# Pair products: background steps bound behind sums and results, low parts written in place

## The chip, the cores and the metric

The kernel runs on one core of a Trainium2 chip. The metric is the device time of one execution in microseconds (us). Three executions of the kernel before took 1269.88 to 1273.23 us, with a median of 1271.97 us.

## The reference

One layer of an encoder trunk, for 1024 tokens of width 1024, all in float32. Cut to what matters:

```python
h    = rmsnorm(x) * g_pre_mix
proj = h @ w_in                       # 512 columns each: u_pool, q, k, v
# pooling: 4 groups of 128 columns, trailing windows of 2, 4, 8, 16 tokens
pooled = window_mean(u_pool) - u_pool            # per group
y_pool = (pooled @ w_pool_mix[g]) * pool_scale   # per group, then @ w_br_pool
# stick-breaking attention, 8 heads of 64, q scaled by 1/8
o_sb  = stick_breaking_attention(q, k, v)        # then @ w_br_sb
gates = sigmoid(h @ w_gate + b_gate)             # 2048 columns
m     = (gates[:, :1024] * y_pool + gates[:, 1024:] * y_sb) @ w_out
x     = x + rmsnorm(m) * g_post_mix
h2    = rmsnorm(x) * g_pre_mlp
out   = x + rmsnorm(relu(h2 @ w_up)**2 @ w_down) * g_post_mlp
```

## The kernel before, in words

Each float32 operand is split into a high and a low part in a rounded float32 format, and a product is the sum of three matmuls: high by high, low by high, high by low (lines 110 to 112). The phases follow one another: the norm and the first projections (u_pool and v), then the **pair stage** in `phase_project`, which the change touches, then attention, the output products and the MLP.

**Pair products.** The pair stage computes the gates and q and k. The list `PAIRS` has twelve pairs of weight blocks in this order: gates 0 to 4, q0, k0, q1, k1, gates 5 to 7. By a scheme of Winograd's kind a pair takes seven products (b11, b21, t2, t3, t1, t4, b22) rather than eight, each of twelve matmuls into one PSUM bank of 128x512, so 84 products. The operands on the activation side (h_hi, ht_hi and their like in the profile) are ready; those on the weight side are prepared pair by pair.

**Sums and results.** `begin` copies b11 to the tile u on ScalarE (line 683) and adds b21 to get c11 (line 684). The other sums, on VectorE (lines 695 to 705), make u, v and c22 from the products, always in float32 tiles of 128x512; u has two buffers and c11, v and c22 one each. Four of these tiles are results of a pair. `result` (from line 534) takes them on: a gate's result is put through the sigmoid in place on ScalarE and stored from ScalarE's DMA queue to gscr. A result of q or k is scaled and rounded to its high part on ScalarE (line 542), its low part is made on VectorE (line 543), both in a staging tile with room for the two (`staged`: the tags m0 and m1 in turn), and GpSimd's DMA queue stores them to qscr.

**Banks.** `newbank` deals the PSUM banks out in a cycle over three tags with 2, 2 and 3 buffers, so that a bank comes round after six or nine products. In the profile these banks are named sw.

**Weights.** `sw_weights` (from line 505) is a generator, advanced by one step after each product of the pair in front. It loads two raw tiles of 512 KB from SyncE's queue (wraw, with two buffers, and wrawx, with one), and splits them: the high part is a cast on ScalarE (line 1193), the low part a subtraction on VectorE (line 1194). Three sums of raw blocks (lines 519, 521 to 523) come between. The parts of a1 and sa are named whi and wlo in the profile, those of a22 a0hi and a0lo or a1hi and a1lo, those of sb s0hi, s0lo, s1hi, s1lo, by odd and even pair.

**Background steps.** `later` (from line 551) is a second generator, for work that is not of the pairs. One step of it is traced after each product, and one more after every sixth product among the first 36. It begins with four pooling groups. For a group it loads u on ScalarE's queue (line 560), builds the window sums by doubling (lines 581 and 582, tiles named win), makes the mean less u (lines 586 to 590), splits that (ph on ScalarE, line 594, and pq on VectorE, line 595), multiplies it by the group's mixing matrix into the bank dm and one more bank of the cycle, scales both into win and u (line 602 on ScalarE, line 603 on VectorE) and stores these to yscr from GpSimd's queue (line 610). All its big tiles share four buffers of 512 KB, tags m0 to m3. Then come eight value steps: each loads a tile of values and its neighbour shifted by one token (vpair), subtracts them (line 622), splits the difference (line 625 on ScalarE, line 626 on VectorE) and stores it to sscr (line 627). The value steps work in the tags m2 and m3 (m0 and m1 for two of them), so that m0 and m1 are free for the staging tiles of q and k.

**What sets the order.** Work is traced in the order of the program, and a scheduler then puts each engine's instructions in an order by its own simulated timeline. On the chip each engine, and each DMA queue, executes in that order; what stands behind a waiting instruction waits too. `tc.issue_after(ins)` (with a helper named `behind`) ties what is traced under it: on the engine of `ins` it stands behind `ins` in the order. In the kernel before, the pair stage ties nothing of the background and of the weights in this way. After the last pair the first head's tiles are loaded into the same four buffers, and attention begins.

## Time and profile before

| | value |
|---|---|
| median of 3 executions | 1271.97 us (1269.88 to 1273.23) |
| the profiled execution's own time | 1273.34 us |
| its span in the profile | 1271.3 us |
| TensorE (PE) busy | 1241.4 us, 98% |
| VectorE (DVE) busy | 967.8 us, 76% |
| ScalarE (ACT) busy | 631.0 us, 50% |
| GpSimd (POOL) busy | 179.7 us, 14% |
| chain that ended last | PE 69%, DVE 13%, DMA 10%, issue 5%, ACT 3% |

The profile is one execution, taken by the hardware profiler. A row of its groups gives the line and engine, the operation with the tiles it writes and reads, its count, the time it was busy, the mean of one, and the idle time ahead of it with what ended most of that. In a table by stretch the columns after the stretch are its length, then the busy time of PE, PE's weight loads, DVE, ACT and POOL, each with its number of instructions in brackets; then the clock granted to PE as a share of the full one, the mean busy share of the sixteen DMA engines, and GB/s. In a row of a timeline the start and the duration stand first, and in square brackets the time that the instruction's engine waited and for what. Rows of waits give the waiting operation, what it waited for, and total, count and longest. Rows of DMA issues give the queue, the count, the size of one, and the median time from issue to landing.

### The profile page before, as it was taken

Reading aid. Unit: us, or ns where it says so; the run is one execution under the profiler, and the core shown is the slowest. Engines: PE = TensorE matmul, PEld = TensorE weight load, DVE = VectorE, ACT = ScalarE, POOL = GpSimd, SP = SyncE. Lnnn points to the kernel's source line nnn. Section 1 sums busy time; section 2 is a strip of 40 time slices with the busy share of each in tenths; the row PEclk is TensorE's granted clock in tenths of the full one; section 3 lists DMA queues with packets and bytes.
Section 4 is the critical chain, followed back from the end, with each engine's and each line's share of the span. In section 5 each row is a group of like instructions: output and inputs, shape, how many; then the busy total and the mean of one; then the engine's idle time right before and its main releaser. Section 6 shows DMA issues by size and latency. Waiting matters only on the chain.

```text
span 1271.3 us, 16191 instructions
## 1 busy us (share of the span) xinstructions
PE 1241.4 (98%) x5707; PEld 1020.3 (80%) x5707; DVE 967.8 (76%) x1311; ACT 631.0 (50%) x1010; POOL 179.7 (14%) x319
## 2 busy tenths in 40 slices
PE   9999999998999999999999999999999999999998
PEld 6887778877877888787778878888888888888887
DVE  8849687766578898877797879887865565776975
ACT  8147334333456666674556546455454443344452
POOL 1212112342101111101100002222121110001000
PEclk9999999999999999999999999999999999999999
DMA  6586878977899674457648677676559996556552
GB/s 218 172 226 165 249 189 252 314 240 247 294 359 345 203 213 118 117 129 219 215 135 263 198 248 257 226 241 221 180 182 335 306 300 229 197 198 248 191 198 67
DMA packets 110305, 283.00 MB, mean 223 GB/s; under 512 B 12464, under 2 KB 17584, under 8 KB 109072
## 3 DMA queue, kind: packets, MB, share of 16 engines
q1 hardware_dynamic: 65696, 165.28, 37.9%
q0 software_dynamic: 30992, 91.13, 25.1%
q10 hardware_dynamic: 13536, 25.57, 6.2%
q8 instruction: 45, 0.74, 0.2%
q14 instruction: 36, 0.29, 0.1%
HBM read 208.52 MB, written 94.37 MB: 238 GB/s over the span
## 4 chain that ended last, share of the span: by engine, by line
PE 69%; DVE 13%; DMA 10%; issue 5%; ACT 3%; POOL 0%; ACTq 0%; SPq 0%; DVEq 0%; POOLq 0%
PE d L110 15%; PE d L111 15%; PE d L112 15%; PE sw L110 3%; PE sw L111 3%; PE sw L112 3%; PE o L838 2%; DVE T L801 2%; PE dbr L111 2%; PE dbr L112 2%; PE dbr L108 2%; DVE wlo L78 1%; DMA yscr<-win 1%; DMA wraw<-w 1%; PE at L814 1%
## 5 line engine op out<-in xcount | busy, mean ns | idle before, releaser
L111 PE MATMUL d<-blo,whi 128*128 128x512 f32 (+1 forms) x456 | 172.3, 378 | 0.0
L112 PE MATMUL d<-bhi,wlo 128*128 128x512 f32 (+1 forms) x456 | 171.9, 378 | 0.0
L110 PE MATMUL d<-bhi,whi 128*128 128x512 f32 (+1 forms) x456 | 168.7, 378 | 0.0
L112 PEld LDWEIGHTS d<-bhi,wlo 128*128 128x128 f32 x456 | 85.8, 188 | 16.1
L111 PEld LDWEIGHTS d<-blo,whi 128*128 128x128 f32 x456 | 85.7, 188 | 15.8
L110 PEld LDWEIGHTS d<-bhi,whi 128*128 128x128 f32 x456 | 85.5, 188 | 16.0
L801 DVE TENSOR_TENSOR_SCAN T<-T,past 128x512 f32<-128x512 f32 (+3 forms) x64 | 84.8, 1345 | 8.7 <-ACT T L799 8.4
L111 PE MATMUL d<-b_lo,whi 128*128 128x512 f32 x196 | 76.2, 390 | 1.2 <-DVE b_lo L1085 1.2
L110 PE MATMUL d<-b_hi,whi 128*128 128x512 f32 x196 | 75.7, 390 | 0.1
L112 PE MATMUL d<-b_hi,wlo 128*128 128x512 f32 x196 | 74.2, 389 | 0.0
L78 DVE TENSOR_TENSOR wlo<-wraw,whi 128x1024 fp32r<-128x1024 f32 x45 | 54.9, 1220 | 15.2 <-ACT whi L76 13.5
L76 ACT CAST whi<-wraw 128x1024 fp32r<-128x1024 f32 x45 | 47.5, 1056 | 37.9 <-DMA wraw<-w 19.0
L1382 DVE TENSOR_TENSOR wlo<-slots_hi,whi 128x1024 fp32r<-128x1024 f32 x29 | 35.5, 1223 | 37.3 <-ACT whi L1380 37.3
L1380 ACT CAST whi<-slots_hi 128x1024 fp32r<-128x1024 f32 x29 | 30.5, 1051 | 67.2 <-PE d L111 61.0
L799 ACT ACTIVATE T<-z 128x256 f32<-128x256 f32 (+2 forms) x96 | 44.8, 492 | 38.1 <-PE z L797 34.9
L1380 ACT CAST whi<-slots_lo 128x1024 fp32r<-128x1024 f32 x27 | 28.4, 1054 | 60.6 <-PE d L111 50.3
L110 PE MATMUL sw<-h_hi,whi 128*128 128x512 f32 x144 | 56.5, 392 | 1.9 <-DVE c L684 1.3
L111 PE MATMUL sw<-h_lo,whi 128*128 128x512 f32 x144 | 56.1, 389 | 0.0
L112 PE MATMUL sw<-h_hi,wlo 128*128 128x512 f32 x144 | 55.5, 390 | 0.1
L824 ACT CAST ahi<-at 128x512 fp32r<-128x512 f32 (+1 forms) x96 | 44.1, 484 | 22.8 <-PE at L814 19.8
L825 DVE TENSOR_TENSOR alo<-at,ahi 128x512 fp32r<-128x512 f32 (+1 forms) x96 | 50.0, 542 | 6.7 <-ACT ahi L824 6.6
L1193 ACT CAST whi<-wraw 128x1024 fp32r<-128x1024 f32 (+1 forms) x29 | 26.7, 928 | 54.7 <-PE d L111 24.2
(447 smaller groups left out, 3451.6 us busy)
## 6 DMA issues: line engine op xcount, KB each, us to landing
wraw<-w SPq DMA_DIRECT2D x57, 512.0 KB, 5.0
ext_b<-ascr SPq DMA_DIRECT2D x40, 512.0 KB, 7.0
wscr<-w POOLq DMA_DIRECT2D x32, 512.0 KB, 9.6
slots_hi<-w SPq DMA_DIRECT2D x10, 1024.0 KB, 8.0
slots_lo<-w SPq DMA_DIRECT2D x10, 1024.0 KB, 8.6
qq<-qscr SPq DMA_DIRECT2D x32, 256.0 KB, 5.1
pscr<-p SPq DMA_DIRECT2D x32, 256.0 KB, 3.9
u<-pscr ACTq DMA_DIRECT2D x32, 256.0 KB, 4.3
```

What stands on the lines that cost most here:

```text
L76: nc.scalar.copy(hi, raw)
L78: self.lows.append(nc.vector.tensor_sub(lo, raw, hi.bitcast(F32)).ins)
L110: nc.tensor.matmul(ps, wh, rh, start=first and i == 0, stop=False)
L111: nc.tensor.matmul(ps, wh, rl, start=False, stop=False)
L112: self.last_mm = nc.tensor.matmul(ps, wl, rh, start=False, stop=last and i == n - 1).ins
L799: self.after = nc.scalar.activation(f, z[:, :n], AF.Sigmoid, scale=-1.0)
L801: nc.vector.tensor_tensor_scan(f[:, ::-1], f[:, ::-1], past[:, ::-1], 1.0, ALU.mult, ALU.max)
L824: self.att_hi = nc.scalar.copy(hi[:, c:], at[:, c:]).ins
L825: self.att_lo = nc.vector.tensor_sub(lo[:, c:], at[:, c:], hi[:, c:].bitcast(F32)).ins
L1193: self.last_hi = nc.scalar.copy(hi, src).ins
L1380: last_split[0] = nc.scalar.copy(hi, src).ins
L1382: last_split[1] = nc.vector.tensor_sub(lo, src, hi.bitcast(F32)).ins
```

## The change

It has three parts, all in the pair stage.

First, the background steps are **bound**: each is now traced under `behind`, once for the last main instruction on ScalarE (the copy of b11 or the last result) and once for the last main sum on VectorE. On these two engines a step's instructions stand behind the copies, results and sums of the products in front. The weights' step comes after it and stays unbound, as it was. The extra background step comes after every fourth of the first 28 products, rather than after every sixth of the first 36.

Second, a **low part** of q or k is no longer made at its result. It is put on a list and made, bound in the same way, after the next product. It is written over its result's own tile (c11, c22, v or u), and stored from there. The staging tile now holds the high parts of two results. A result of q takes six stores of 128 KB in place of two of 256 KB and two of 128 KB, a result of k four of 128 KB in place of two of 256 KB: over the stage 32 more DMAs on GpSimd's queue for the same bytes.

Third, the steps themselves are **cut finer**: ph and pq are two steps, so are the scalings on ScalarE and on VectorE, and so are the subtraction, the high part and the low part of a value step. Some empty steps go in return. And the tiles for the window sums alternate over the tags m1 and m2 from one group to the next (`n = 3 - n`), where they began at m1 in each group.

```diff
--- before.py
+++ after.py
@@ -221,6 +221,7 @@
         self.turn = 0
         self.wq = nc.sync
         self.op7, self.sw, self.heads = {}, {}, {}
+        self.stage, self.lower = [], []
         self.phase_in()
         self.phase_project()
         self.phase_attention()
@@ -535,19 +536,28 @@
         nc = self.nc
         c = slice(h * H, h * H + H)
         if kind == "g":
-            nc.scalar.activation(t, t, AF.Sigmoid, bias=self.vt[:, V_BG + f : V_BG + f + 1], scale=sign)
+            self.act_main = nc.scalar.activation(
+                t, t, AF.Sigmoid, bias=self.vt[:, V_BG + f : V_BG + f + 1], scale=sign
+            ).ins
             return nc.scalar.dma_start(self.gscr[f][:, c], t)
         sc = sign * (0.125 if kind == "q" else 1.0)
-        e = self.staged([P, 2, H], F32R, f"{kind}s")
-        nc.scalar.activation(e[:, 0, :], t, AF.Copy, scale=sc)
-        nc.vector.scalar_tensor_tensor(
-            out=e[:, 1, :], in0=t, scalar=sc, in1=e[:, 0, :].bitcast(F32), op0=ALU.mult, op1=ALU.subtract
-        )
-        for b in range(2):
-            scr, s = self.qscr[kind == "k"][2 * f + b], e[64 * b : 64 * b + 64].bitcast(F32)
-            nc.gpsimd.dma_start(scr[0:128, c].rearrange("(n p) c -> p n c", n=2), s)
-            if kind == "q":
-                nc.gpsimd.dma_start(scr[128:192, c], s[:, 0, :])
+        if not self.stage:
+            e = self.staged([P, 2, H], F32R, f"{kind}s")
+            self.stage = [e[:, 0, :], e[:, 1, :]]
+        hi = self.stage.pop(0)
+        self.act_main = nc.scalar.activation(hi, t, AF.Copy, scale=sc).ins
+
+        def low():
+            nc.vector.scalar_tensor_tensor(
+                out=t.bitcast(F32R), in0=t, scalar=sc, in1=hi.bitcast(F32), op0=ALU.mult, op1=ALU.subtract
+            )
+            parts = (hi.bitcast(F32), t, hi.bitcast(F32)) if kind == "q" else (hi.bitcast(F32), t)
+            for b in range(2):
+                scr = self.qscr[kind == "k"][2 * f + b]
+                for n, e in enumerate(parts):
+                    nc.gpsimd.dma_start(scr[64 * n : 64 * n + 64, c], e[64 * b : 64 * b + 64])
+
+        self.lower.append(low)
 
     def later(self, newbank):
 
@@ -570,13 +580,13 @@
         nc.scalar.copy(wmh, wm)
         nc.vector.tensor_sub(wml, wm, wmh.bitcast(F32))
         yield
+        n = 2
         for g in range(4):
             iu = 3 * (g % 2)
-            u = nxt_u
-            cur, n = u, 0
+            cur = u = nxt_u
             for i in range(g + 1):
                 sh = 1 << i
-                n = 1 + i % 2
+                n = 3 - n
                 nxt = whole(n, name="win")
                 nc.vector.tensor_add(nxt[:, sh:], cur[:, sh:], cur[:, : 1024 - sh])
                 nc.vector.tensor_copy(nxt[:, :sh], cur[:, :sh])
@@ -592,6 +602,7 @@
             sc = self.vt[:, V_PSC + g : V_PSC + g + 1]
             ph, pq = whole(3 - n, F32R, "ph"), whole(3 - iu, F32R, "pq")
             nc.scalar.copy(ph, cur)
+            yield
             nc.vector.tensor_sub(pq, cur, ph.bitcast(F32))
             yield
             yield
@@ -600,6 +611,9 @@
                 c = slice(h * H, h * H + H)
                 self.mm3(d, [(wmh[:, g, :], wml[:, g, :], ph[:, c], pq[:, c])])
                 nc.scalar.activation(cur[:, c].bitcast(F32R), d, AF.Copy, scale=sc)
+            yield
+            for h, d in enumerate(ds):
+                c = slice(h * H, h * H + H)
                 nc.vector.scalar_tensor_tensor(
                     out=u[:, c].bitcast(F32R), in0=d, scalar=sc, in1=cur[:, c], op0=ALU.mult, op1=ALU.subtract
                 )
@@ -608,7 +622,6 @@
             yield
             for t, scr in zip((cur, u), self.yscr):
                 nc.gpsimd.dma_start(scr[:, g, :], t)
-            yield
             yield
         for t in range(NK):
             n = 0 if t in (5, 7) else 2
@@ -621,13 +634,13 @@
             e = p[:, 0, :]
             nc.vector.tensor_sub(e, e, p[:, 1, :])
             e = e.rearrange("p (h x) -> p h x", h=8)
+            yield
             v = self.mx.tile([P, 8, P], F32R, name="vs", tag=f"m{n + 1}")
             nc.scalar.copy(v[:, :, 0:64], e)
+            yield
             nc.vector.tensor_sub(v[:, :, 64:128], e, v[:, :, 0:64].bitcast(F32))
             nc.gpsimd.dma_start(self.sscr[t], v.rearrange("p h x -> p (h x)").bitcast(F32))
-            yield
             if t < 5:
-                yield
                 yield
 
     def sum_pieces(self, behind, n):
@@ -661,18 +674,25 @@
         next(bg)
         count = itertools.count()
         nxt = iter(())
+        self.act_main = self.dve_main = None
 
         def product(w, at, name):
             d = newbank()
             self.half(d, w, at, name)
+            c = next(count)
+            lower, self.lower = self.lower, []
+            with self.behind(self.act_main), self.behind(self.dve_main):
+                for f in lower:
+                    f()
+                for _ in range(2 if c % 4 == 3 and c < 28 else 1):
+                    next(bg, None)
             next(nxt, None)
-            next(bg, None)
-            c = next(count)
-            if c % 6 == 5 and c < 36:
-                next(bg, None)
             if c % 3 == 2 and c < 48:
                 self.sum_piece_with(self.last_mm)
             return d
+
+        def add(out, a, b):
+            self.dve_main = nc.vector.tensor_add(out, a, b).ins
 
         begun = {}
 
@@ -680,8 +700,8 @@
             kind, f = self.PAIRS[i]
             w = self.sw[i]
             u, c11 = part("u"), part("c11")
-            nc.scalar.copy(u, product(w["a1"], 0, "b11"))
-            nc.vector.tensor_add(c11, u, product(w["a1"], 512, "b21"))
+            self.act_main = nc.scalar.copy(u, product(w["a1"], 0, "b11")).ins
+            add(c11, u, product(w["a1"], 512, "b21"))
             self.result(kind, f, 0, c11, 1.0)
             begun[i] = u
 
@@ -692,18 +712,20 @@
             if i not in begun:
                 begin(i)
             u, v, c22 = begun[i], part("v"), part("c22")
-            nc.vector.tensor_add(u, u, product(w["sb"], 0, "t2"))
-            nc.vector.tensor_add(v, u, product(w["sa"], 0, "t3"))
+            add(u, u, product(w["sb"], 0, "t2"))
+            add(v, u, product(w["sa"], 0, "t3"))
             d = product(w["sa"], 512, "t1")
-            nc.vector.tensor_add(c22, v, d)
-            nc.vector.tensor_add(u, u, d)
+            add(c22, v, d)
+            add(u, u, d)
             self.result(kind, f2, 1, c22, -1.0)
             if i == len(self.PAIRS) - 2:
                 begin(i + 1)
-            nc.vector.tensor_add(v, v, product(w["a22"], 0, "t4"))
+            add(v, v, product(w["a22"], 0, "t4"))
             self.result(kind, f2, 0, v, -1.0)
-            nc.vector.tensor_add(u, u, product(w["sb"], 512, "b22"))
+            add(u, u, product(w["sb"], 512, "b22"))
             self.result(kind, f1, 1, u, 1.0)
+        for f in self.lower:
+            f()
         self.run(bg)
         self.v = [
             self.big.tile([P, 4, 8, P], F32R, name=f"v{i}", tag=f"big_{n}1") for i, n in enumerate(("hi", "lo"))
```

Where instructions come to stand shows at three places. The first is ScalarE in pooling group 1, from the high part s1hi of the third pair's weights on. L602 and L613 are the scalings of dm and of the second bank, L560 and L570 the load of the next u; c_ and a number is c11 or c22. Before:

```order
L1193 CAST s1hi<-wrawx 128x1024
L602 ACTIVATE win<-dm,vt 128x512
L560 DMA u<-uscr_121 128x1024
L602 ACTIVATE win<-sw,vt 128x512
L538 ACTIVATE v<-v,vt 128x512
L538 ACTIVATE u<-u,vt 128x512
L539 DMA gscr_74<-v 128x512
L538 ACTIVATE c_1194<-c_1194,vt 128x512
L539 DMA gscr_66<-u 128x512
L539 DMA gscr_67<-c_1194 128x512
L1193 CAST a0hi<-wrawx 128x512
```

After, from the last result ahead of the same scalings:

```order
L539 ACTIVATE u<-u,vt 128x512
L542 DMA gscr_66<-u 128x512
L1215 CAST a0hi<-wrawx 128x512
L1215 CAST whi<-wrawx 128x1024
L613 ACTIVATE win<-dm,vt 128x512
L570 DMA u<-uscr_121 128x1024
L613 ACTIVATE win<-sw,vt 128x512
L1215 CAST s0hi<-wraw 128x1024
```

The scalings and the u load stood ahead of a0hi and of the results of that pair; now they stand behind the results, and behind a0hi and a whi.

The second place is VectorE there, from the low part s1lo on, whose end frees the raw tile wrawx for its next load. L603 and L617 are the second scalings, L581 and L591 window sums. Before:

```order
L1194 TENSOR_TENSOR s1lo<-wrawx,s1hi 128x1024
L603 SCALAR_TENSOR_TENSOR u<-dm,vt,win 128x512
L603 SCALAR_TENSOR_TENSOR u<-sw,vt,win 128x512
L581 TENSOR_TENSOR win<-u 128x1023
L582 COPY win<-u 128x1
L581 TENSOR_TENSOR win<-win 128x1022
L582 COPY win<-win 128x2
L586 SCALAR_TENSOR_TENSOR win<-win,u 128x1020
L589 TENSOR_TENSOR win<-win,rcnt 128x4
L695 TENSOR_TENSOR u<-u,sw 128x512
L590 TENSOR_TENSOR win<-win,u 128x4
L1194 TENSOR_TENSOR a0lo<-wrawx,a0hi 128x512
```

After:

```order
L1216 TENSOR_TENSOR s1lo<-wrawx,s1hi 128x1024
L695 TENSOR_TENSOR u<-u,sw 128x512
L606 TENSOR_TENSOR pq<-win,ph 128x1024
L1216 TENSOR_TENSOR a0lo<-wrawx,a0hi 128x512
L520 TENSOR_TENSOR wrawx<-wrawx 128x512
L522 TENSOR_TENSOR wrawx<-wraw,wrawx 128x512
L523 TENSOR_TENSOR wraw<-wraw,wrawx 128x512
L524 TENSOR_TENSOR wraw<-wraw 128x512
L1216 TENSOR_TENSOR wlo<-wrawx,whi 128x1024
L695 TENSOR_TENSOR u<-u,sw 128x512
L617 SCALAR_TENSOR_TENSOR u<-dm,vt,win 128x512
L617 SCALAR_TENSOR_TENSOR u<-sw,vt,win 128x512
```

Eleven rows lay between s1lo and a0lo, most of them the pooling steps of two groups; now there are two, and the pooling steps stand behind the weight's.

The third place is VectorE around the second pair of keys. L543 and L551 are the low parts of results, and c_ with a number is c11 or c22. Before:

```order
L703 TENSOR_TENSOR v<-v,sw 128x512
L543 SCALAR_TENSOR_TENSOR ks<-c_2384,ks 128x512
L1194 TENSOR_TENSOR a0lo<-wraw,a0hi 128x512
L543 SCALAR_TENSOR_TENSOR ks<-v,ks 128x512
L519 TENSOR_TENSOR wraw<-wraw 128x512
L705 TENSOR_TENSOR u<-u,sw 128x512
L521 TENSOR_TENSOR wraw<-wrawx,wraw 128x512
```

After (all sums have line 695 there, since one helper makes them):

```order
L695 TENSOR_TENSOR v<-u,sw 128x512
L695 TENSOR_TENSOR c_2396<-v,sw 128x512
L695 TENSOR_TENSOR u<-u,sw 128x512
L635 TENSOR_TENSOR vpair<-vpair 128x512
L695 TENSOR_TENSOR v<-v,sw 128x512
L695 TENSOR_TENSOR u<-u,sw 128x512
L551 SCALAR_TENSOR_TENSOR c_2396<-c_2396,ks 128x512
L551 SCALAR_TENSOR_TENSOR v<-v,ks 128x512
L551 SCALAR_TENSOR_TENSOR u<-u,ks 128x512
```

The low parts stood between the last two sums; now they stand behind the last sum, and they write c_2396, v and u themselves.

## The prediction

> **What bounds the kernel now.** I read the page first, then the busy times by stage, then what TensorE (PE) waited for in the stage that the change touches, and last the rows of the engines behind those waits.
>
> ```profile
> span 1271.3 us, 16191 instructions
> PE 1241.4 (98%) x5707; PEld 1020.3 (80%) x5707; DVE 967.8 (76%) x1311; ACT 631.0 (50%) x1010; POOL 179.7 (14%) x319
> ```
>
> PE is busy for 98% of the span, so a faster VectorE (DVE) or ScalarE (ACT) is worth only the PE idle time that it takes away. The change touches the pair stage, 97 to 346 us. The next rows give busy time and instruction counts by stretch; the last one is a stretch in which PE never stops.
>
> ```profile
> 97.00:207.00 110.00, 104.93 (x450) 83.10 (x449) 95.20 (x143) 53.85 (x75) 20.85 (x27) 1.00 0.75 202
> 207.00:311.00 104.00, 98.84 (x426) 80.24 (x425) 71.93 (x104) 36.48 (x52) 34.59 (x60) 0.98 0.85 275
> 311.00:346.00 35.00, 35.00 (x156) 29.00 (x155) 21.08 (x30) 13.81 (x18) 5.23 (x10) 1.00 0.80 277
> 900.00:1100.00 200.00, 200.00 (x884) 165.62 (x883) 126.10 (x134) 87.36 (x105) 24.37 (x34) 1.00 0.81 255
> ```
>
> 200 us for 884 matmuls is 0.226 us each, or 2.71 us for a product of twelve. At that pace the three stretches need 101.8, 96.4 and 35.3 us. The first, with the pooling steps, loses 8.2 us; the second, with the query and key pairs, 7.6; the third nothing. **15.8 us is all that this change can win.** In the first stretch DVE is busy for 95 of 110 us: time in which it stands still is soon missing to PE. What PE waited for in the whole stage:
>
> ```profile
> PE sw L110 <- DVE u L705: 3.3, 1, 3.3
> PE sw L110 <- ACT whi L1193: 2.6, 2, 1.5
> PE sw L110 <- DVE c L684: 1.3, 1, 1.3
> PE sw L110 <- DVE u L695: 0.8, 2, 0.4
> ```
>
> Two kinds: sums that are late, so that no PSUM bank is free, and weight splits that are late. The longest is this, by PE's timeline:
>
> ```profile
> 298.70 0.39 PE L112 MATMUL sw<-h_hi,wlo 128*128 128x512 f32 x1
> 302.41 0.77 PE L110 MATMUL sw<-ht_hi,a1hi 128*128 128x512 f32 x1 [3.32 <-DVE u L705]
> 305.93 0.40 PE L112 MATMUL sw<-ht_hi,a1lo 128*128 128x512 f32 x1
> 306.17 0.40 PE L110 MATMUL sw<-ht_hi,a1hi 128*128 128x512 f32 x1
> ```
>
> The next matmul starts 3.71 us later, 3.5 too late, and the eight steps from 302.41 to 305.93 take 3.52 us where 1.81 is usual: together 5.2 of the 7.6 us. Why the sum was late shows on ACT and DVE:
>
> ```profile
> 294.64 0.63 ACT L542 ACTIVATE ks<-c 128x512 fp32r<-128x512 f32 x1 [4.50 <-DMA qscr<-qs]
> 299.80 0.63 ACT L542 ACTIVATE ks<-v 128x512 fp32r<-128x512 f32 x1 [3.95 <-DMA qscr<-ks]
> 300.46 0.69 DVE L543 SCALAR_TENSOR_TENSOR ks<-v,ks 128x512 fp32r<-128x512 f32 x1 [3.87 <-ACT ks L542]
> 301.68 0.68 DVE L705 TENSOR_TENSOR u<-u,sw 128x512 f32<-128x512 f32 x1
> ```
>
> ACT waits for a store to free a staging tile, DVE's low part waits for ACT, and the sum that frees the bank stands behind it in DVE's queue.
>
> **The change part by part.** *Query and key results.* The transfers of the stage, each with its size and median time from issue to landing:
>
> ```profile
> wraw<-w SPq DMA_DIRECT2D x14, 512.0 KB, 7.2
> wrawx<-w SPq DMA_DIRECT2D x8, 512.0 KB, 8.7
> qscr<-qs POOLq DMA_DIRECT2D x16, 256.0 KB, 4.8
> u<-uscr ACTq DMA_DIRECT2D x4, 512.0 KB, 6.3
> yscr<-win POOLq DMA_DIRECT2D x4, 512.0 KB, 7.9
> qscr<-qs POOLq DMA_DIRECT2D x16, 128.0 KB, 4.7
> ```
>
> Before, results took two staging tiles in turn, so each waited for the store of the result two before it; the last three of a pair come one product after the other, which leaves 5.4 us for a store that lands 4.8 after its issue at the median. Now a tile holds the high parts of two results. The shortest return is from the second result of a pair to the first of the next, four products or 10.9 us, against 0.7 for the cast, four issues and 4.7 for the landing, about 8. ACT's wait goes, and the low parts stand behind the sums in the order shown above. Of 7.6 us I count 5.5 won; 2.1 stay for the load in the next part.
>
> New is that a low part keeps its result's buffer until its store has landed, and the sum of the next pair that writes there waits for it. For the buffer v: one product until the last sum (2.7), some 2 us for sums, cast and low part, up to twelve stores ahead on POOL, 4.7 for the landing. The price of an issue:
>
> ```profile
> L550 POOL DMA_DIRECT2D qscr<-qs x16 | 8.6, 542 | 13.5 <-ACT qs L542 13.5
> ```
>
> That makes 2.7 + 2 + 12 x 0.54 + 4.7 = 15.9 us, and v is written again five products (13.6 us) later. DVE is 2.3 us late, but a bank comes round only after six products, so PE has five products of slack; I count nothing, and 2.3 for each of three pair changes (7) if that slack is spent. The 32 more stores take 17 us of POOL, which was busy for 34.6 of 104 us and serves only stores here: nothing. The bytes are the same.
>
> *Pooling.* Removed: the first window sum of a group no longer needs the tile that the group before is storing. It cost this:
>
> ```profile
> 127.86 1.22 DVE L1194 TENSOR_TENSOR s1lo<-wrawx,s1hi 128x1024 fp32r<-128x1024 f32 x1
> 129.66 0.75 DVE L603 SCALAR_TENSOR_TENSOR u<-sw,vt,win 128x512 fp32r<-128x512 f32 x1
> 137.26 1.23 DVE L581 TENSOR_TENSOR win<-u 128x1023 f32<-128x1023 f32 x1 [6.86 <-DMA yscr<-win]
> 138.66 1.22 DVE L581 TENSOR_TENSOR win<-win 128x1022 f32<-128x1022 f32 x1
> 141.80 0.69 DVE L1194 TENSOR_TENSOR a0lo<-wrawx,a0hi 128x512 fp32r<-128x512 f32 x1
> ```
>
> DVE stood for 6.86 us, and under that wait the load for a0lo landed unseen. Now this cover is gone: with the pooling steps bound, DVE comes to a0lo about 2 us after s1lo, whose end frees the tile for the load, and ACT has a0hi ahead of the two scalings of dm and of the u load. The loads of this stretch, one row for each window named:
>
> ```profile
> wraw<-w SPq DMA_DIRECT2D x1, 512.0 KB, 3.5
> wraw<-w SPq DMA_DIRECT2D x1, 512.0 KB, 4.7
> wrawx<-w SPq DMA_DIRECT2D x1, 512.0 KB, 8.9
> wraw<-w SPq DMA_DIRECT2D x1, 512.0 KB, 7.0
> ```
>
> They were issued at 125.1, 113.2, 129.1 and 187.7 us. The 8.9 one shared the DMA engines with a u load and two yscr stores; in the new order these come behind it, so the other three are nearest, and I take 5.5, with 3.5 and 8.9 as ends. Then: s1lo ends at 129.0, the load lands at 134.6; a0hi 0.6, three DVE steps of 0.6, a cast of 1.05 and one scaling 0.7 put the u load at 138.7 and the last step on dm's bank at 141.4. PE, which needs that bank at 141.0, loses 0.4. The u load lands at 145.0 (6.3); one window sum and the sum for v end at 146.9, and PE needs v's bank at 144.2: 2.7. Two more steps of 1.1 (a weight split, the second window sum) and two sums later, at 150.5, c22's bank is free, wanted at 149.2: 1.3. Group 1 loses 4.4 us. Groups 2 and 3 have the same chain with more products done ahead; I count 1.5 for both, 0.9 for the start, which is unchanged, and 1.0 of small change: **7.8 against 8.2.** The 6.86 us wait is gone, but a wait for a load takes its place.
>
> *Value steps* keep their work and DMAs; the last is bound to product 80 of 84, before the stage ends. *The start of attention*: SP now issues all weight loads before the first head's, which before stood in front of three of them. Nothing counted. *Loads of weights* keep their number.
>
> The Trainium skill has a figure that bears on this: in "DMA: Bandwidth & Descriptors", section "Anatomy of one DMA", a DMA takes about 2.0 us and then its bytes at 436 GB/s, an estimate of 3.2 us for a load of 512 KB. The stage's medians of 7.2 and 8.7 us don't agree; by it the time would be that of the first rival.
>
> **Sum.** The profiled execution took 1273.3 us (span 1271.3 and 2.0 around it); 5.5 + 0.4 is 5.9 less, 1267.4. The median of the runs shown is 1.4 below the profiled one; 1272.0 less some 5.5 (the 0.4 is below what such a walk can tell) gives **1266.5 us**.
>
> **The rivals.**
>
> *Quick loads.* If loads land in 3.5 us, as the quickest row has it, group 1 loses 2 us less, the other groups 1.5 and the query stage some 0.5: 4 us less, 1262.5. For it: the chain thins out its own traffic. Against it: the medians.
>
> *Slow loads, slower than before.* If a load that DVE has come to takes the 8.9 us of the row above, each such chain is 3.4 us longer: in groups 1, 2 and 3 that reaches PE (10.2), in the query stage, with its slack, some 1 us. 11 us on top of 1266.5 is 1277.5. It decides from about 7.2 us on, the median of wraw, where 1.7 x 3 + 0.5 eats the gain. For it: those medians. Against: their company in the old order.
>
> *The gain is given back at the start of attention.*
>
> ```profile
> 330.00:346.00 16.00, 16.00 (x72) 13.26 (x71) 7.76 (x12) 5.16 (x7) 2.17 (x4) 1.00 1.01 365
> 346.00:360.00 14.00, 13.87 (x70) 11.41 (x68) 7.16 (x11) 4.58 (x10) 0.00 (x0) 1.00 1.04 379
> 360.00:380.00 20.00, 18.34 (x103) 15.25 (x100) 17.25 (x30) 12.94 (x34) 2.42 (x9) 1.00 1.00 357
> ```
>
> From 330 to 380 us the DMA engines are full (shares of 1.01, 1.04 and 1.00). If what has to be moved there, and not PE, sets when attention runs, a stage that ends 5.5 us earlier only waits longer: 1272. For it: full shares, and the first head's load now comes later. Against it: PE is busy for 13.87 of 14 us at the change-over, so it has work there. The same time results if the buffers' new wait costs its 7 us and the pooling wins a little.
>
> **How the numbers follow.** Forecast 0.45; quick loads 0.12; given back 0.23; slow loads 0.20. A measurement of this kernel tells about 0.3%, 3.8 us, from no change. The forecast lies 5.5 us below the median with some 3 either way, so three quarters of it count as faster: 0.34 + 0.12 is 0.46. Same: 0.23 and the rest of the forecast, 0.33. Slower: the slow loads and a little of the given-back case, 0.21. The range runs from 1260.5 (quick loads, and the query stage's last 2 us won as well) to 1278 (the slow loads); the forecast's own is 1263 to 1270.
>
> **What would show it.** In the profile after: no ACT wait over 1 us for a qscr store, and no PE wait near 3 us in the query pairs (the first step); sums that wait there for qscr stores instead, without a PE wait behind them (slack); DVE waits of 3 to 5 us ahead of a0lo for a load and 1 to 4 ahead of the first window sum for u, no longer for yscr (the pooling chain); a loss against PE's pace of about 8 us up to the query pairs and 2 after them. Wrong would be a loss of 12 or more in the pooling stretch, a PE wait for sums behind qscr stores, or a PE wait of several us between 340 and 380.

## The result, and the profile after

The changed kernel takes **1283.55 us** (median of four executions, 1280.73 to 1284.95) against 1270.93 for the kernel before; the ratio is 1.0101 (95% interval 1.0081 to 1.0121). It is 12.6 us slower, where 5.5 us faster was forecast, and it lies above the range. The profiled execution took 1284.95 us.

The head of the page of the changed kernel, then its waits of TensorE (PE) in the pair stage (total, count, longest, in us):

```profile
span 1282.9 us, 16204 instructions
PE 1244.4 (97%) x5707; PEld 1024.6 (80%) x5707; DVE 971.6 (76%) x1311; ACT 630.5 (49%) x1010; POOL 193.6 (15%) x351
```

```profile
PE sw L110 <- ACT u L703: 8.9, 1, 8.9
PE sw L110 <- DVE win L600: 3.0, 1, 3.0
PE sw L110 <- DVE v L695: 2.0, 2, 1.5
PE sw L110 <- DVE c L695: 1.0, 1, 1.0
PE sw L110 <- ACT s1hi L1215: 1.0, 1, 1.0
```

The wait of 3.3 us for L705 is gone, and one of 8.9 us has come. To compare the stages, I cut both profiles at the same counts of products on PE: the first of the pair stage, the 36th (before the change the first of q0), the 64th (the first of g5), the end of the last, and the first matmul of the output products behind attention. The changed kernel takes a few products of neighbouring pairs in another order, so there the names of the stages hold to within a product or so. Busy times by these stretches, before and then after:

```profile
97.40:206.40 109.00, 103.93 (x445) 82.26 (x445) 94.20 (x141) 53.45 (x74) 20.85 (x27) 1.00 0.75 202
206.40:284.80 78.40, 76.68 (x338) 62.66 (x337) 54.87 (x81) 27.76 (x40) 28.21 (x49) 1.00 0.88 287
284.80:347.70 62.90, 59.46 (x253) 48.45 (x254) 39.28 (x54) 23.36 (x31) 11.61 (x21) 0.97 0.78 265
```

```profile
0.00:98.70 98.70, 95.42 (x405) 75.94 (x406) 70.54 (x112) 46.29 (x76) 19.12 (x33) 0.98 0.65 198
98.70:209.20 110.50, 103.67 (x439) 83.71 (x438) 91.04 (x135) 51.53 (x71) 19.68 (x25) 0.97 0.75 205
209.20:298.10 88.90, 80.01 (x344) 65.67 (x344) 62.84 (x90) 31.27 (x44) 40.34 (x77) 0.94 0.78 247
298.10:356.50 58.40, 57.83 (x254) 47.23 (x253) 36.77 (x52) 21.39 (x29) 14.29 (x27) 1.00 0.74 257
356.50:400.00 43.50, 38.34 (x199) 30.91 (x197) 29.67 (x46) 21.40 (x54) 2.83 (x11) 1.00 0.95 345
```

Taking 0.2262 us for each product and mixing matmul from a stretch's length gives what PE lost there. This table has it for both kernels and for the runs that follow; "attention" is the length from the end of the pair stage to the output products.

| profiled execution | pooling, lost | q0 to k1, lost | g5 to g7, lost | pair stage | attention | span |
|---|---|---|---|---|---|---|
| before | 8.6 | 2.3 | 5.9 | 250.2 | 226.0 | 1271.3 |
| changed | 11.5 | 11.4 | 1.3 | 257.6 | 229.9 | 1282.9 |
| e1_pe_order | 16.8 | 0.2 | 4.6 | 255.0 | 228.9 | 1278.4 |
| e2_low_back | 9.6 | 0.2 | 0.1 | 243.4 | 240.7 | 1279.8 |
| e3_unbound | 10.1 | 8.2 | 3.0 | 254.7 | 235.8 | 1285.5 |
| e4_low_only | 10.3 | 3.2 | 10.0 | 256.9 | 226.2 | 1276.3 |
| e5_old_steps | 5.4 | 6.8 | 4.0 | 249.7 | 226.0 | 1269.3 |
| e6_fine_only | 9.4 | 5.2 | 4.6 | 252.7 | 224.7 | 1274.0 |
| e7_one_pin | 10.9 | 11.8 | 1.5 | 257.6 | 229.4 | 1280.8 |
| e8_pin_late | 9.3 | 7.5 | 4.8 | 255.1 | 227.4 | 1277.7 |
| e9_weights_bound | 5.9 | 0.2 | 0.1 | 239.6 | 231.3 | 1265.6 |
| e10_k1_bound | 9.1 | 3.9 | 8.8 | 255.2 | 231.6 | 1281.9 |
| e11_v_two | 9.8 | 9.2 | 0.1 | 252.5 | 248.5 | 1295.1 |
| e13_bound_low_back | 6.3 | 3.9 | 0.1 | 243.7 | 229.7 | 1268.5 |
| e14_bound_early | 5.5 | 0.2 | 3.3 | 242.4 | 245.6 | 1283.3 |
| e15_bound_old_steps | 4.1 | 3.6 | 6.8 | 247.9 | 238.2 | 1281.4 |
| e17_bind_pool | 8.6 | 9.6 | 7.6 | 259.2 | 234.4 | 1286.9 |
| e18_sums_early | 14.6 | 1.3 | 0.5 | 249.8 | 232.6 | 1276.5 |
| e20_bound_44 | 6.2 | 0.2 | 0.1 | 239.9 | 239.6 | 1274.3 |
| e21_idle_products | 7.5 | 0.2 | 0.1 | 246.6 | 224.4 | 1265.4 |

Each row is a single execution. That of e5 was the fastest of ten (1271.31 us, median 1275.59) and that of e6 the slowest of ten (1275.77, median 1270.45), so their rows do not stand for their medians.

The 11.6 us between the two spans are 7.4 in the pair stage, 3.9 in attention, 1.3 ahead of the pair stage and 1.0 less behind attention. The 1.3 are not the change's: 405 matmuls stand there in both, PE's clock was granted at 0.98 in the changed kernel and 1.00 in the one before, and the runs with 97.4 to 97.8 us ahead of the pair stage (e7, with the whole change, is one) and with 98.3 to 99.4 do not sort by any part of the change.

The 9 us at q1, by the timelines of PE, ScalarE (ACT) and VectorE (DVE):

```profile
256.65 0.39 PE L112 MATMUL sw<-ht_hi,wlo 128*128 128x512 f32 x1
265.93 0.80 PE L110 MATMUL sw<-h_hi,s1hi 128*128 128x512 f32 x1 [8.89 <-ACT u L703]
266.52 0.63 PE L111 MATMUL sw<-h_lo,s1hi 128*128 128x512 f32 x1
```

```profile
260.01 0.62 ACT L1215 CAST a0hi<-wrawx 128x512 fp32r<-128x512 f32 x1 [11.10 <-DMA wrawx<-w]
264.35 1.04 ACT L1215 CAST s0hi<-wraw 128x1024 fp32r<-128x1024 f32 x1 [3.72 <-DVE wraw L524]
265.30 0.58 ACT L703 COPY u<-sw 128x512 f32<-128x512 f32 x1
```

```profile
240.64 0.69 DVE L635 TENSOR_TENSOR vpair<-vpair 128x512 f32<-128x512 f32 x1 [4.12 <-DMA vpair<-vscr]
...
242.46 0.68 DVE L551 SCALAR_TENSOR_TENSOR v<-v,qs 128x512 fp32r<-128x512 f32 x1
...
250.53 1.22 DVE L1216 TENSOR_TENSOR s1lo<-wrawx,s1hi 128x1024 fp32r<-128x1024 f32 x1
251.67 1.22 DVE L1216 TENSOR_TENSOR wlo<-wraw,whi 128x1024 fp32r<-128x1024 f32 x1
260.66 0.69 DVE L1216 TENSOR_TENSOR a0lo<-wrawx,a0hi 128x512 fp32r<-128x512 f32 x1 [7.77 <-ACT a0hi L1215]
261.38 0.69 DVE L520 TENSOR_TENSOR wrawx<-wrawx 128x512 f32<-128x512 f32 x1
...
265.42 1.22 DVE L1216 TENSOR_TENSOR s0lo<-wraw,s0hi 128x1024 fp32r<-128x1024 f32 x1 [1.17 <-ACT s0hi L1215]
266.57 0.68 DVE L695 TENSOR_TENSOR v<-u,sw 128x512 f32<-128x512 f32 x1
```

Read from below: the last row is the sum of **k0's** product t3, whose matmuls were over at 240.7. It stands behind the splits of the weights of **k1**, the second pair after k0. The split a0lo waits for its load, which s1lo, at 250.53, had only just made possible. The load took this long from issue to landing:

```profile
wrawx<-w SPq DMA_DIRECT2D x1, 512.0 KB, 8.2
```

On ACT the copy of q1's b11 stands behind the same split. Six products after b11 and after t3 their banks are wanted again, and PE stops. Behind the stall its steps take 0.43 us for some 4 us (the clock granted from 260.1 to 270.4 us was 0.50), which is the other 2.2 of the 11.3 us lost at q1.

The first two rows of DVE tell of the buffer v, which k0's sum needs too. The low part of q0 that is made in v stood behind a value step, which waited 4.1 us for its load. The last store from v was issued at 245.39 and landed 6.0 us later, at 251.4. So v was free 10.7 us after the end of t3, yet 5.5 us before PE wanted t3's bank (256.9), and DVE stood still from 252.9 to 260.7. The held buffer by itself would not have stopped PE here; the order did.

### The profile page after: what moved, and what is told of

Its sections match the earlier page's. It is cut to its first block, busy times and chain, and to the rows that moved or that the text cites. A ratio compares the mean times of both kernels' runs of the same rounds, so it can differ in the third digit from the quotient of the medians.

```text
span 1282.9 us, 16204 instructions
## 1 busy us (share of the span) xinstructions
PE 1244.4 (97%) x5707; PEld 1024.6 (80%) x5707; DVE 971.6 (76%) x1311; ACT 630.5 (49%) x1010; POOL 193.6 (15%) x351
## 4 chain that ended last, share of the span: by engine, by line
PE 65%; DVE 13%; DMA 11%; issue 8%; ACT 3%; POOL 0%; SPq 0%; ACTq 0%; DVEq 0%; POOLq 0%
PE d L110 15%; PE d L112 15%; PE d L111 15%; DMA wraw<-w 2%; PE o L860 2%; PE dbr L111 2%; PE dbr L112 2%; PE dbr L108 2%; DVE T L823 2%; PE at L836 1%; PE sw L110 1%; PE sw L111 1%; DVE wlo L78 1%; PE sw L112 1%; DMA vpair<-vscr 1%
## 5 line engine op out<-in xcount | busy, mean ns | idle before, releaser
L112 PEld LDWEIGHTS d<-bhi,wlo 128*128 128x128 f32 x456 | 85.8, 188 | 15.8
L1215 ACT CAST whi<-wraw 128x1024 fp32r<-128x1024 f32 (+1 forms) x29 | 26.9, 932 | 58.1 <-PE d L111 23.9
```

What stands on the lines that cost most here:

```text
L112: self.last_mm = nc.tensor.matmul(ps, wl, rh, start=False, stop=last and i == n - 1).ins
L1215: self.last_hi = nc.scalar.copy(hi, src).ins
```

## The experiments

### Is it PE's order? (e1, e7, e8)

PE's own order had changed too. Before, PE took q1 as b11, b21, t2, t3, t1, t4, b22; now it takes b11, b21, t3, half of b22, t2, t1, t4, the rest of b22. With b22 fourth, b11's bank is wanted three products earlier. The first theory was that this spends the slack.

```diff
-            self.half(d, w, at, name)
-            c = next(count)
+            with self.behind(self.pe_main): self.half(d, w, at, name)
+            self.pe_main, c = self.last_mm, next(count)
```

> The changed kernel with one addition: on TensorE every product stands behind the product traced before it. In the changed kernel's trace PE takes q1 as b11, b21, t3, half of b22, t2, t1, t4, and stalls 9.05 us ahead of b22, whose bank is that of b11. Order theory (PE comes to a bank three products early, so the late weight split on ACT and DVE is no longer covered): the stall at q1 falls to 2 us or less, the pair stage from 257.8 us to about 248, the time to 1271 to 1275. Load theory (the weight loads come too late whatever PE's order): 5 us or more stay at q1 or move to the next product, and the time is 1279 or more.

1280.14 us, ratio 1.0066 (1.0039 to 1.0093). The query-key stretch lost 0.2 us, as the theory had it; pooling lost 16.8, which no theory had. But the scheduler had changed ACT's and DVE's orders as well, and the copy of q1's b11 was no longer late (0.4 us behind its product). So this run does not tell the two apart. The next ties one product alone (`self.pe_main if next(self.np) == 55 else None`) and leaves the other engines' orders as they were, but for a row or two.

> The changed kernel with one product tied: q1's b22 stands on TensorE behind q1's t4. The orders of ACT and DVE stay those of the changed kernel but for a row or two, so b11's copy should come as late as there (13.9 us after the end of its product). Order theory: PE now has three products (8 us) between t3 and b22, so the 11.3 us lost at q1 fall to 1 to 4, the query-key stretch from 88.8 to 79 to 82 us, and the time to 1273 to 1277. Load theory (late splits cost this whatever PE's order): 8 us or more of the 11.3 stay in q1 or k1, and the time stays at 1281 or more.

1284.17 us, ratio 1.0116 (1.0097 to 1.0135): nothing was won, and q1 lost 11.7 us. PE now stops, again after b11, b21 and t3, ahead of t2, whose bank is that of k0's t3. PE and DVE of this run:

```profile
265.06 0.77 PE L110 MATMUL sw<-ht_hi,s1hi 128*128 128x512 f32 x1 [9.62 <-ACT whi L1215]
```

```profile
258.33 0.69 DVE L1216 TENSOR_TENSOR a0lo<-wrawx,a0hi 128x512 fp32r<-128x512 f32 x1 [7.51 <-ACT a0hi L1215]
264.23 0.68 DVE L695 TENSOR_TENSOR v<-u,sw 128x512 f32<-128x512 f32 x1
```

PE starts 0.15 us after the sum into v ends (the releaser that the row names, whi, was long done). **The order theory fell.** What holds PE here is the sum on DVE; the late copy on ACT, which released PE in the changed kernel, is the other branch of the same split.

Tying all products from q0 on (the condition is `next(self.np) >= 36`) was less than hoped:

> The changed kernel with TensorE's products tied to their traced order from q0 on alone (the pooling stretch stays free, unlike in the run that tied all). Order theory: pooling stretch 110.5 us as in the changed kernel, query-key stretch 76 to 78, g5 to g7 58 to 62. If attention then takes the changed kernel's 229.9 us, the time is 1270 to 1274; if what attention waits for is moved at its own pace (the given-back theory), the stretch after it takes 235 us or more and the time is 1277 or more.

1281.13 us, ratio 1.0088 (1.0073 to 1.0103). The stall at q1 is gone, but one of 5.5 us, for the split of a pooled tile, lies in q0, and one of 2.9 in g5. A tie on one engine makes the scheduler deal all engines' orders anew.

### The three parts, one undone or one alone (e2 to e6)

e2 makes the low parts at their results again, in staging tiles for one result, with the larger stores:

```diff
-        if not self.stage:
-            e = self.staged([P, 2, H], F32R, f"{kind}s")
-            self.stage = [e[:, 0, :], e[:, 1, :]]
+        e = self.staged([P, 2, H], F32R, f"{kind}s")
+        # ... both parts, and the stores, as before
```

> The changed kernel with the low parts as before: made at the result, in a staging tile for one result, with the two or four larger stores; background bound, steps cut finer. PE's order at q1 is then the traced one again. Order theory: the 11 us at q1 go, the waits of ACT for qscr stores come back in k1 and g5 with some 6 us, so the time is about 1278. Load theory (binding alone makes the loads late): q1 keeps 5 us or more, and the time is 1284 or more.

1281.62 us, ratio 1.0085 (1.0058 to 1.0111). Neither theory: q1 lost nothing, and the staging wait did not come back to PE either, so the pair stage took 243.4 us, 6.8 less than before. Attention took 14.7 us more and ate it all. So the loss at q1 came with the low parts in place.

e3 takes the background steps out of `behind` and leaves the low parts in it:

```diff
-                for _ in range(2 if c % 4 == 3 and c < 28 else 1):
-                    next(bg, None)
+            for _ in range(2 if c % 4 == 3 and c < 28 else 1):
+                next(bg, None)
```

> The changed kernel with the background steps not bound; the low parts stay in place and bound, the steps cut finer. Order theory and load theory both take the 11 us at q1 away here (PE's order is the traced one, and the weight split no longer stands behind bound value steps); the pooling loses some 8 us as before: 1268 to 1272. Store theory (32 more stores and held buffers make the loads slow and the sums late): a stall of 5 us or more stays between q1 and g5, 1278 or more.

1286.73 us, ratio 1.0105 (1.0067 to 1.0142). A miss: the wait at q1 is under 1 us, but one of 4.8 has come at k1, and attention is 9.8 us longer than before.

e4 has only the second part (so its low parts are not bound), e6 only the third, both in the kernel before; e5 is the changed kernel without the third. The new place of the extra step goes with the third part in e5 and e6.

```diff
             self.half(d, w, at, name)
+            lower, self.lower = self.lower, []
+            for f in lower:
+                f()
             next(nxt, None)
```

> The kernel before with the low parts in place and after the next product, nothing bound, old steps. The prediction's first term alone: the staging wait goes and 5.5 to 7.6 us are won, 1264 to 1267, if held buffers cost nothing. Store theory: the sums that wait for stores give it back, 1271 or more, with DVE waits for qscr in k0 to g5.

1277.23 us, ratio 1.0040 (1.0025 to 1.0054). **The second part, alone and not bound, is a loss.** The staging wait is gone, and 8.9 us are lost from 315 to 330 us. There DVE comes to the sum into v late, held for its store, and then to a value step that waits for its load with three more sums behind it:

```profile
318.15 0.69 DVE L707 TENSOR_TENSOR v<-u,sw 128x512 f32<-128x512 f32 x1 [0.91 <-DMA qscr<-v]
323.53 0.69 DVE L630 TENSOR_TENSOR vpair<-vpair 128x512 f32<-128x512 f32 x1 [4.69 <-DMA vpair<-vscr]
```

```diff
-            for _ in range(2 if c % 4 == 3 and c < 28 else 1):
+            for _ in range(2 if c % 6 == 5 and c < 36 else 1):
```

(e5; with the steps of `later` as before. e6 has the same line the other way round.)

> The changed kernel with the third part undone: background bound, low parts in place, but the pooling and value steps cut as before, and the window tiles from m1 in each group. The prediction's view, that the tiles in turn remove a wait of 6.9 us on the pooling path: the pooling stretch grows from 110.5 to 114 to 118 us. If the finer cut is of no account, it stays at 109 to 112. TensorE's order has still more permutations here, so the chain theory expects 5 us or more lost in the query-key stretch too: 1282 to 1292.

1275.59 us, ratio 1.0039 (1.0022 to 1.0056), 8 us better than the changed kernel. The pooling stretch took 104.5 us, where more than 110.5 were expected: in the company of the binding, the finer cut, the tiles in turn and the extra step's new place **cost** 6 us, as far as the fastest execution of e5 can tell.

> The kernel before with the finer steps, the window tiles in turn and the extra step after every fourth product; nothing bound, low parts as before. If the finer steps and tiles are what the pooling stretch gains (the 6.9 us wait for a yscr store goes), it takes 104 to 107 us and the time is 1266 to 1269; by the prediction's chain of loads it takes 108 to 110 and the time is 1270 to 1273. The query-key stretch and g5 to g7 should be as before, 78 and 63 us.

1270.45 us, ratio 0.9995 (0.9979 to 1.0010). Alone the third part is worth nothing; pooling took 109.8 us, 0.8 more than before. Neither the second nor the third part wins anything alone; the first alone was not run. Undoing any one of the three leaves the kernel slower than before.

### The chain on DVE (e9, e10, e11, e17, e18)

The theory now: an unbound weight split has come to stand ahead of sums that PE waits for, and its load sets when they run. e9 binds the weights' steps too, e10 only those for k1.

```diff
                     next(bg, None)
-            next(nxt, None)
+                next(nxt, None)
```

> The changed kernel with the weights' steps bound as well, behind the last copy or result on ACT and the last sum on DVE. The high part that waits for the load then comes behind the copies and sums in front of it. Load theory: the copy of q1's b11 is at most 4 us behind its product, no PE wait over 2 us in the pooling or query-key stretches, pooling 105 to 108 us, query-key 76 to 78. Order theory says the same of q1, but that the pooling stretch stays at 109 to 112, since there PE's order has other permutations. Attention 226 to 230: 1265 to 1272; given-back theory: 235 or more, and 1275 or more.

1267.62 us, ratio 0.9985 (0.9974 to 0.9996). Pooling lost 5.9 us, and from q0 to the end of the stage PE lost 0.3. DVE now has the sum into v ahead of the split, and the split no longer waits, though its load took 7.8 us:

```profile
240.10 1.23 DVE L1216 TENSOR_TENSOR s1lo<-wrawx,s1hi 128x1024 fp32r<-128x1024 f32 x1
241.24 0.68 DVE L695 TENSOR_TENSOR v<-u,sw 128x512 f32<-128x512 f32 x1
...
252.44 0.68 DVE L1216 TENSOR_TENSOR a0lo<-wrawx,a0hi 128x512 fp32r<-128x512 f32 x1
```

Here s1lo ended at 241.3 and a0lo began at 252.4: eleven microseconds, in which DVE did eleven other instructions. In the changed kernel there was one.

```diff
-            next(nxt, None)
+            k1 = 49 <= c < 56
+            with self.behind(self.act_main if k1 else None), self.behind(self.dve_main if k1 else None): next(nxt, None)
```

> The changed kernel with one stretch of the weights bound: the steps that prepare k1's weights (traced after q1's products) stand behind the last copy or result on ACT and the last sum on DVE. The new theory from the run with one pin: q1's stall is a chain on DVE; the sum of k0's t3 is held until the store of q0's low part has left v, the unbound weight split a0lo of k1 has come to stand ahead of that sum, and it waits 8 to 9 us for its load; PE's order stays the changed kernel's here. Chain theory: the 11.3 us at q1 fall to 2 or less, the query-key stretch from 88.8 to 77 to 80 us. Held-buffer theory (the store alone makes the sum late): 5 us or more stay. Time by the chain theory 1273 to 1277.

1283.09 us, ratio 1.0086 (1.0058 to 1.0115). At q1 11.3 us became 2.0. The time did not follow: two pairs on, in g5, where the splits are unbound, the same chain stands again, with g6's split ahead of k1's sum:

```profile
290.43 1.23 DVE L1217 TENSOR_TENSOR s1lo<-wraw,s1hi 128x1024 fp32r<-128x1024 f32 x1
294.82 0.70 DVE L1217 TENSOR_TENSOR a0lo<-wraw,a0hi 128x512 fp32r<-128x512 f32 x1 [3.16 <-ACT a0hi L1216]
...
300.67 0.68 DVE L696 TENSOR_TENSOR v<-u,sw 128x512 f32<-128x512 f32 x1
```

```profile
301.50 0.77 PE L110 MATMUL sw<-ht_hi,s1hi 128*128 128x512 f32 x1 [5.48 <-DVE v L696]
```

Is the held buffer a part of the chain? In the changed kernel the sum into v cannot run before the stores of q0's low part have left v, at 251.4. e11 gives v a second buffer: `bufs=1 + (name in "uv")`.

> The changed kernel with two buffers for v in place of one, so that k0's sum into v waits for no store of q0; weights unbound as in the changed kernel. Chain theory: without the held buffer the sums stand ahead of a0lo in DVE's order, so q1 loses 2 us or less and the query-key stretch takes 77 to 80 us. If the weights' loads alone are the cause, 5 us or more stay at q1 or k1. Time by the chain theory 1272 to 1277; the pooling stretch stays near 110.

1296.19 us, ratio 1.0193 (1.0171 to 1.0216). A miss: 9.0 us stayed at q1 and k1. The chain itself had gone, since k0's sum ran at 249.1, ahead of a0lo. Another of its kind stood there, a value step ahead of q1's sum for c11:

```profile
271.39 0.69 DVE L635 TENSOR_TENSOR vpair<-vpair 128x512 f32<-128x512 f32 x1 [6.70 <-DMA vpair<-vscr]
272.00 0.68 DVE L695 TENSOR_TENSOR c<-u,sw 128x512 f32<-128x512 f32 x1
```

So with the buffer no longer held the scheduler puts the sum ahead of the split. That the hold is what put it behind is inferred from this one order, since the scheduler's own timeline is not on record. The instruction that waits here, the value step, is a bound one, so binding alone does not keep such an instruction away from the sums. Is the binding of the value steps the cause? e17 binds the pooling alone (`on = c < 35`).

> The changed kernel with steps and low parts bound only up to the 35th product, that is with the pooling bound and the value steps and low parts free. DVE's order around k1's a0lo is still the chain (s1lo, wlo, a0lo, then k0's sums). Chain theory: q1 still loses 8 to 11 us, the query-key stretch takes 86 to 90. If the bound value steps (their wait for a load of 4 us, ahead of the weights) are the cause, q1 loses 4 or less. Time by the chain theory 1279 to 1287.

1291.35 us, ratio 1.0162 (1.0133 to 1.0192). q1 lost 9.5 us, so the bound value steps are not the cause at q1. Last, the length of the load: e18 takes the weight sums out of the stretch (`c % 2 == 1 and c < 32`).

> The changed kernel with the sixteen pieces of weight sums (wscr, 512 KB DRAM to DRAM on POOL's queue) traced after every second product up to the 32nd, not after every third up to the 48th, so that none runs in the query-key stretch. DVE's order around k1's a0lo is as in the changed kernel, with k0's sums behind it. If the load's length decides (8.15 us from issue to landing in the changed kernel, with two wscr pieces issued just ahead of it): the load takes 5 to 6.5 us and the stall at q1, 9.05 us there, falls to 5.5 to 7.5. If it is of no account, the stall stays at 8.5 to 10. The time may go either way, since the pooling stretch gets the pieces: 1278 to 1286.

1278.57 us, ratio 1.0058 (1.0034 to 1.0082). The load took 5.4 us in place of 8.2, and q1 lost 1.1 us in place of 11.3. So the fall was larger than expected, and not the load's alone: the load was also issued 2.7 us earlier, PE came 2.8 later, after losing 3.1 more in the pooling stretch, and the sum into v stands ahead of s0lo here, behind it in the changed kernel. Counted from the start of q1's first product the load landed after 11.2 us in the changed kernel, 10.5 in e7, 8.8 in e17 and 2.9 in e18, and PE lost 9.1, 9.8, 6.7 and 1.0 us at the stall itself; the rest of the 11.3, 11.7, 9.5 and 1.1 is the slow steps behind a long stall. In three of the four the stall is the landing less some 2 us, in e7 less 0.7.

### What the parts are worth with the weights bound (e13, e15)

> Background and weights bound, finer steps, low parts as before (made at the result, staging tile for one result). Compared with the run with the weights bound (1267.6), it shows what the low parts in place are worth. If the staging wait of the kernel before comes back: 5 to 6 us more in the query-key stretch and g5 (134.6 us for both there), 1271 to 1275. If binding the weights alone ends it: 134 to 137, 1265 to 1269.

(e2 with the weights bound.) 1270.41 us, ratio 1.0001 (0.9985 to 1.0016): 2.8 us above e9, with intervals that overlap. 3.9 us are lost in the query-key stretch, 3.0 of it at k1.t2, and ACT there waits for stores to qscr again. So the low parts in place are worth some 3 us in this company, as far as two runs so close can tell.

> Background and weights bound, low parts in place, but the pooling and value steps cut as before and the window tiles from m1 in each group. The run with the changed kernel and old steps took 104.5 us for the pooling stretch and 226.0 for attention, in place of 110.5 and 229.9. If the old steps give both with the weights bound too: pooling 102 to 105, query-key and g5 to g7 134 to 138, attention 226 to 228, 1259 to 1264. If with the weights bound the steps do not matter: pooling 105, attention 231, 1266 to 1269.

(e9 with the old steps.) 1283.03 us, ratio 1.0096 (1.0069 to 1.0123). The pooling stretch is as short, 103.6 us, but g5 to g7 lost 6.8 and attention 12.2 more than before. The old steps' short attention of e5 did not carry over.

### Attention (e14, e20, e21)

e9 won 10.6 us of the pair stage and gave back 5.3 in attention. Its last value tile was stored 9.6 us before the end of the pair stage, where the kernel before had it at 23.9, and the loads for attention stand behind it. e14 and e20 let the value steps end earlier (`c < 60`, `c < 44`).

> The kernel with the weights bound as well, and the extra background step kept up to the 60th product, not the 28th, so that the value steps end some eight products earlier. Entry theory (attention starts late since the bound value steps end late, and the first head's and the y loads stand behind them): the last store of values is issued before 316 us (329 without it), the last load of values lands at most 16 us after the pair stage's end (19.5), attention takes 226 to 228 us (231.3), and the time is 1261 to 1265. Given-back theory (what has to be moved sets the end): attention stays at 231 or more and the time at 1266 to 1269.

> The kernel with the weights bound as well, and the extra background step up to the 44th product (28th there, 60th in the run that lost 14 us at the entry). Entry theory: the last store of values is issued 15 us or more before the end of the pair stage (9.6 with 28), attention takes 226 to 229 us, the time is 1262 to 1266. If the entry follows no such rule, attention takes 233 or more, as with the 60th, and the time is 1270 or more.

1284.83 us, ratio 1.0109 (1.0088 to 1.0131), and 1276.26, ratio 1.0041 (1.0025 to 1.0058). The last values were stored 21.9 and 15.2 us ahead, and attention took 245.6 and 239.6. **This theory fell.** e21 adds to e9 work for PE that nobody reads:

```diff
+        with self.behind(self.last_mm):
+            for _ in range(2):
+                self.half(newbank(), w["sb"], 512, "b22")
         for f in self.lower:
             f()
```

> The kernel with the weights bound as well, and 24 matmuls (two products, 5.4 us) added on TensorE behind the last product, into banks that nobody reads. Given-back theory: at the start of attention PE waits for what is moved, which does not come later because of the added work, so the time stays within 1.5 us of that kernel's 1267.6 and the stage from the added matmuls' end to the output products shrinks from 231.3 to 226 to 228. If PE's own work sets the entry, the time is 1272 to 1274.

**1265.30 us, ratio 0.9958 (0.9944 to 0.9973).** 5.4 us of matmuls for nothing, and the kernel is no slower; its median is 2.3 us below e9's, and attention took 224.4 us, both somewhat beyond what the given-back theory had expected. The stretch from the end of the pair stage to 400 us, of e9 and of e21:

```profile
338.50:400.00 61.50, 54.11 (x279) 44.31 (x279) 44.03 (x71) 32.16 (x82) 5.88 (x20) 0.97 0.94 337
```

```profile
345.40:400.00 54.60, 52.51 (x280) 43.02 (x279) 43.20 (x70) 31.44 (x81) 5.87 (x20) 1.00 0.93 337
```

By 400 us both have done the same matmuls (279 and 280). PE started seven microseconds later in e21 and waited that much less, at the same 337 GB/s. So in e9 PE's own work does not set the start of attention, as the prediction's third rival has it; for the changed kernel this was not tried. That the transfers set it is argued from their share (0.93 to 0.94) and not shown: no run changed them alone, and the longest waits of PE that the trace names in this stretch of e9 are for DVE and ACT, 2.1 us at most. The added matmuls changed the orders at the start of attention as well, so their own part in the 2.3 us is open.

In e2, where attention lost most beside e11 and e14, ACT's queue shows one way in which a late transfer may reach PE. The store of a gate is issued 6.3 us after the end of its result, and the first exponentials of attention (T) stand behind it:

```profile
343.99 0.72 ACT L539 ACTIVATE v<-v,vt 128x512 f32<-128x512 f32 x1 [0.47 <-DVE v L688]
350.99 0.33 ACTq L542 DMA_DIRECT2D gscr<-v  x1
351.37 0.72 ACT L539 ACTIVATE u<-u,vt 128x512 f32<-128x512 f32 x1 [6.65 <-DMA ylo<-yscr]
```

The releaser named is a load on another queue, of y for attention, which landed at 350.9. That the store waited for it is inferred from this and was not tried. What makes attention take 224.7 us in one kernel (e6) and 248.5 in another (e11), with the same work in it, stays open.

## Why the prediction was wrong

- **What bounds the kernel** was right, and so was the cap of 15.8 us (16.8 by the cuts used here): no run got the pair stage's loss below 6.2. That a shorter pair stage is a shorter kernel was not: e2 won 6.8 us there and e9 10.6, and attention took 14.7 and 5.3 of them back.
- **The staging wait**: the wait itself was right. From k1 to the end of g7 the kernel before lost 8.1 us, the changed one 1.3, and ACT waits for no qscr store there. But as a gain in time it shows only beside bound weights (e9 against e13, 2.8 us). Alone and not bound, the edit costs 5.4 us (e4).
- **The step that failed** is the pair of sentences "DVE is 2.3 us late, but a bank comes round only after six products, so PE has five products of slack; I count nothing" and, of a slow load, "in the query stage, with its slack, some 1 us". Each was costed against a free DVE. The hold was mis-sized: v came free 10.7 us after k0's t3, not 2.3, with 4.1 of it a value step's wait for its load, where "some 2 us" had been counted for sums, cast and low part. It was still within the slack. But k0's sum stood behind a split that waits for a load of 8.2 us, in an order that by e11 came of the hold, and both delays came out of the same slack. 2.1 us were counted to stay in the query stage for the load, and 11.4 were lost from q0 to k1, 11.3 of them at q1. None of the signs of being wrong that the prediction names came; what came, a copy and a sum behind a weight split, was not on its list. By the Trainium skill ("DMA: Bandwidth & Descriptors", section "Anatomy of one DMA"), whose fit is for transfers that GpSimd issues, the load would be an estimated 3.2 us; this one was issued on SP and the trace has 8.2, so the measurement decides.
- The rival **slow loads** had the mechanism ("a load that DVE has come to") and nearly its point: it was to decide from 7.2 us on. It had the wrong place. It put 10.2 us into the pooling groups and 1 into the query stage; pooling lost 2.9 more than before, the query stage 9.1. That its 1277.5 us comes nearest to the measured time is therefore luck in the main. In four of eleven pairs of the changed kernel at most two DVE instructions lie between the split that frees a raw tile (s0lo or s1lo) and the one that waits for its next load (a0lo or a1lo), in the kernel before in one (in group 1 ten rows lay between them there, not eleven); I followed the chain in one of them.
- **Pooling**: 7.8 us were forecast, 11.5 measured, and they lie elsewhere. The chain in group 1 came as drawn: DVE waited 5.2 us for a0lo, behind a load of 6.3. But PE lost 0.1 us from 128 to 160 us, where 4.4 were counted. The largest loss, 6.2 us from 182 us on, begins at a sum into v that waits for the store of a gate, 9.3 us under way, and half of it is slow steps behind that wait:

```profile
185.04 0.69 DVE L695 TENSOR_TENSOR v<-u,sw 128x512 f32<-128x512 f32 x1 [2.54 <-DMA gscr<-v]
```

```profile
185.88 0.76 PE L110 MATMUL sw<-ht_hi,s0hi 128*128 128x512 f32 x1 [3.04 <-DVE win L600]
```

The row names win, but the sum ended 0.15 us before PE went on, as in e7, so I take the sum to have held it. No run tried this wait by itself. That the wait for yscr goes was right in the main (6.9 us became 1.2). That the new order is worth the cover it loses was not: with the old steps the same binding loses 5.4 (e5).

- **The start of attention**: "nothing counted", 3.9 us measured. The value steps end later and the loads follow them, but e14 and e20, on e9, show that this does not explain the number, and its cause stays open.

## What to carry to other kernels

Binding one stream of background work behind the main one changes what the unbound streams stand next to: here, with the low parts in place, the loss of PE from q0 on went to 0.3 us only in kernels that bind the weights too (e9, e20, e21), and not in all of those (10.4 us in e15). When an order moves an instruction that waits for a load closer to the one that frees the load's tile, count what DVE does between the two (eleven instructions in e9, one in the changed kernel) and list every result queued behind. And costs that are "within the slack" have to be added up before the slack is compared with them, since they come out of the same few banks.

## What the runs showed of the hardware

- A load of 512 KB on SP's queue, into the same tile at the same place, took 8.2 us in the changed kernel, with two pieces of weight sums (512 KB, DRAM to DRAM) under way beside it, and 5.4 us in e18 without them. The mean busy share of the DMA engines does not tell the two apart: it was 0.66 over the slow load and 0.79 over the quick one.
- Behind a wait of PE of 8.9 us the clock granted was 0.50 until 270.4 us and the steps took 0.43 us rather than 0.23, which cost 2.2 us more; behind the wait of 3.0 us in the pooling groups it was 0.50 too, from 185.0 to 191.8 us, and cost 2.9 more.
- 24 added matmuls at a point where the DMA engines were 0.93 to 0.94 busy cost nothing (e21 against e9).
- In e2 a store on ACT's queue was issued 6.3 us after the end of its result, 0.1 us after a load on SP's queue had landed that the program does not tie it to, and the next instruction on ACT waited too. The tie is inferred.
